# Weight sums in DRAM for fourteen pairs of the first MLP, and a later time for those of the second

## The chip, the cores and the metric

The kernel runs on one core of a Trainium2 chip. The metric is the device time of one execution in microseconds (us); the verdicts compare medians of runs. A core has a matrix engine (TensorE, PE in the profile), three engines for elementwise work (VectorE or DVE, ScalarE or ACT, GpSimd or POOL), a queue engine that issues transfers (SyncE or SP), and sixteen DMA engines that all queues share. Engines run their instructions in program order and wait for each other by semaphores.

## The reference, cut to what matters

Two decoder layers over 512 tokens of width 1024. Layer 0 mixes by a gated convolution beside differential attention, layer 1 by stick-breaking attention. Both then attend into 256 memory tokens and go through a gated MLP of inner width 2816 with a causal convolution of three taps.

```python
for l in range(DEPTH):                       # DEPTH = 2
    h = rmsnorm(x, norm_mix[l])
    x = x + (even_mixer(h, ...) if l % 2 == 0 else odd_mixer(h, ...))
    x = x + mem_attention(rmsnorm(x, norm_xattn[l]), rmsnorm(mem, norm_mem[l]), ...)
    x = x + conv_ffn(rmsnorm(x, norm_ffn[l]), ffn_w_up[l], ffn_conv[l], ffn_w_down[l])

def conv_ffn(h, w_up, w_conv, w_down):
    u = causal_dwconv(h @ w_up, w_conv)      # 1024 -> 2 * 2816
    gate, val = jnp.split(u, 2, axis=-1)
    return (jax.nn.silu(gate) * val) @ w_down
```

All of it is float32.

## The kernel before

**Products.** Activations lie transposed in SBUF, eight chunks of 128 features by 512 tokens. A float32 product is made of three products of a rounded part (`hi`) and its rest (`lo`): hi x hi, hi x lo, lo x hi, each a matmul of 128 x 128 weights with 512 columns. Weights come from DRAM in slots of 128 x 1024 (512 KB). ACT casts a slot into `hi`, DVE subtracts to get `lo`; three raw slots (`raw`) and five of each part (`hi`, `lo`) can be held.

**Pairs in the MLP.** The up-projection goes in 22 pairs, U0 to U21: column block j of the gate and block 22 + j of the value, 8 chunks deep. As whole matmuls a pair takes 2 x 8 x 3 = 48 of 512 columns. For the pairs in `SEVEN` the pair is cut into 2 x 2 blocks (two column blocks by odd and even chunks, and the tokens in two halves) and made of seven products instead of eight (`lin_halved`), each of 12 matmuls with 256 columns: 84. The sums of the token halves are made once per MLP (`fold`). The sums of the weight blocks are made in one of two ways:

- on DVE (`prep_halved`, last part): two slots are loaded, `a` and `r`; four additions of 128 x 512 in the raw slots (L454) give the sums, and the seven left operands are split from there.
- in DRAM, for the pairs in `SUMMED` (`sums_in_dram`): SP's queue copies the pair's four blocks from `wts` to a buffer `dr` in DRAM (1 MB); then three accumulating DMAs on POOL's queue (L508), each waiting for the one before, add blocks onto it. The pair is later loaded in four pieces (`halved_loads`): `a` (512 KB) and `d` (256 KB) from `wts`, `b` and `c` (512 KB each) from `dr`.

`SUMMED[l][j]` names a group of products: the sums of pair j of layer l may begin when the first column block of that group has been planned. In the kernel before, the second MLP has fourteen such pairs, with their sums between U8 of the first MLP and U1 of the second; the first MLP has none, and twelve pairs with DVE's sums. Pairs 12 and 14 of the first MLP are whole.

**Order of the work.** The program is written by a planner (`Issue`). Each piece of work is a generator with a priority; the planner keeps an estimated time for each engine and appends the operation that can start first. An engine's order is thus fixed at build time. Loads have priority 3.0 and the sums 6.0 (`SUMS`), the last. A transfer on SP costs the planner 0.5 us of SP, then 1.7 us, its bytes at 358 GB/s behind the transfers planned before, and 1.0 us. An accumulating DMA costs 1.0 us of POOL and lands 10 us later (`land`). It does not count as load on the DMA engines.

**POOL** also makes the inverse square roots (`rpow`, an operation with `mhalf`): of the norms, of the attention's heads and of the query norms. It clears small tiles in the stick-breaking attention.

**Order of groups**: V, QK0, A0, QK1, A1, A2 (input projection of layer 0 with its attention between), EO0, EO1 (its output projection), KV0 to KV3 (keys and values of the memory), Q0, Q1, XO0, XO1 (cross-attention), the MLP (`FFN_ORDER`: U0 to U21 with D00 to D21 of the down-projection between), then layer 1: SQK0, SV0, SQK1, SQK2, SV1, SQK3, SO0, the KV groups, SO1, Q0, Q1, XO0, XO1, MLP.

The lines of the profile: L492 is every matmul, L496 every transposition on PE, L439 ACT's copies and casts, L442 ACT's other operations, L454 two-input operations on DVE (and the root on POOL), L462 and L472 DVE's operations with scalars, L482 reductions, L501 every DMA on SP's queue, L508 the accumulating DMAs, L514 and L519 POOL's fills.

Of the kernel before, what the change touches and what calls it, by code (L numbers as in the profile page):

```python
# [36 lines left out]

UP_SCALED = 6
FFN_ORDER = [('u', 0), ('u', 1), ('u', 2), ('u', 3), ('u', 4), ('u', 5), ('u', 6), ('u', 7), ('d', 0, 0), ('u', 8), ('d', 0, 1), ('u', 9), ('u', 10), ('d', 0, 2), ('u', 11), ('u', 12), ('d', 0, 3), ('u', 13), ('u', 14), ('u', 15), ('u', 16), ('d', 1, 0), ('u', 17), ('d', 1, 1), ('u', 18), ('d', 1, 2), ('u', 19), ('u', 20), ('d', 1, 3), ('u', 21), ('d', 2, 0), ('d', 2, 1)]
SEVEN = {0: (8, 9, 10, 11, 13, 15, 16, 17, 18, 19, 20, 21), 1: (8, 9, 10, 11, 12, 13, 14, 15, 16, 17, 18, 19, 20, 21)}  # L40

SUMMED = {0: {}, 1: {8: 'U8_0', 9: 'U10_0', 10: 'U12_0', 11: 'U14_0', 12: 'U16_0', 13: 'U18_0', 14: 'U20_0', 15: 'SQK0', 16: 'SQK1', 17: 'SQK2', 18: 'SQK3', 19: 'Q0_1', 20: 'XO0_1', 21: 'U1_1'}}


def weight_groups():
# [61 lines left out]
LOW7 = {GN[n] for n in ()}  # L107
ADDED = {GN[f"U{j}_{l}"]: GN[after] for l in SUMMED for j, after in SUMMED[l].items()}
HALVED = {GN[f"U{j}_{l}"] for l in SEVEN for j in SEVEN[l]}
NSLOT = [len(g[3]) * len(g[4]) * P // SLOT for g in GROUPS]  # L110
# [279 lines left out]
def trunk(ctx: ExitStack, tc: tile.TileContext, xT: bass.AP, memT: bass.AP, wts: bass.AP, par: bass.AP, outT: bass.AP):  # L390
# [1072 lines left out]
    def ffn(l, xin, xout, last):  # L1463
# [40 lines left out]
        def up_done(j):  # L1504
            def done(m, ps):
                gate = m % 2 == 0
                u = ps
                if j < UP_SCALED:
                    u = yield AL(pC)
                    yield Until(lambda: "rrow" in N)  # L1510
                    yield tt(u, ps, N["rrow"], ALU.mult)
                    free(ps)
                t = yield AL(pG)
                yield from conv3(u, f"ffn_conv{l}", j if gate else 22 + j, 44, t)
                free(u)
                if gate:
                    yield act(t, t, AF.Silu)
                    gate_t[j] = t
                    F["silu", l] = F.get(("silu", l), 0) + 1
                else:  # L1520
                    yield Until(lambda: j in gate_t)
                    yield tt(t, t, gate_t[j], ALU.mult)
                    free(gate_t[j])
                    if 4 <= j < 16 or j > 19:
                        q = pHS if j < 16 else pG
                        hi, lo = yield [AL(q, F32R), AL(q, F32R)]
                        o, w = (hi, lo), (hi, lo)
                    else:
                        y = yield AL(pH, F32R, (P, 2, S))
                        o, w = (y[:, 0, :], y[:, 1, :]), (y,)  # L1530
                    yield from split(o[0], o[1], t)
                    free(t)
                    own[j] = w
                    acts[j] = o
            return done

        def up(j):
            done = up_done(j)
            if j in SEVEN[l]:
                acc = yield AL(aACC)  # L1540
# [329 lines left out]
```

## Time and profile before

| | |
|---|---|
| median of 3 runs | 1476.64 us (1476.16 to 1477.26) |
| profiled execution, and its span | 1476.87 us, 1475.1 us |
| busy in the span: PE, DVE, ACT, POOL | 1467.7, 1145.3, 786.4, 103.0 us |
| DMA packets moved | 186.74 MB, mean 127 GB/s |
| of them by accumulating DMAs (queue q0) | 14.68 MB, 6.4% of the sixteen engines' time |
| first halved product to last down-projection, MLP 0 and MLP 1 | 219.0 and 217.4 us |

Busy times of engines overlap. A wait is put down to the semaphore that came last. Rows of the chain or of a timeline begin with the start and the duration in us; rows of groups end with the busy time, the mean of one in ns and the idle time of the engine before them. A `q` behind an engine's name is its sequencer. The granted clock was full (1.00) in the stretches that are used here.

### The profile page before, as it was taken

Reading aid. Unit: us, or ns where it says so; the run is one execution under the profiler, and the core shown is the slowest. Engines: PE = TensorE matmul, PEld = TensorE weight load, DVE = VectorE, ACT = ScalarE, POOL = GpSimd, SP = SyncE. Lnnn points to the kernel's source line nnn. Section 1 sums busy time; section 2 is a strip of 40 time slices with the busy share of each in tenths; the row PEclk is TensorE's granted clock in tenths of the full one; section 3 lists DMA queues with packets and bytes.
Section 4 is the critical chain, followed back from the end, with each engine's and each line's share of the span. In section 5 each row is a group of like instructions: output and inputs, shape, how many; then the busy total and the mean of one; then the engine's idle time right before and its main releaser. Section 6 shows DMA issues by size and latency. Waiting matters only on the chain.

```text
span 1475.1 us, 20895 instructions
## 1 busy us (share of the span) xinstructions
PE 1467.7 (100%) x7904; PEld 1267.0 (86%) x7904; DVE 1145.3 (78%) x1923; ACT 786.4 (53%) x1303; POOL 103.0 (7%) x181
## 2 busy tenths in 40 slices
PE   9999999999999999999999999999999999999998
PEld 7888888888888989999888888888888889999897
DVE  7689766665898887888778989967657996888683
ACT  6576446453554344444577877855535653545341
POOL 2210000000000010000011111001000000000000
PEclk9999999999999999999999999999999999999999
DMA  7122445311333565656334443353244433455351
GB/s 237 58 86 73 131 141 172 114 58 58 100 101 128 133 170 156 171 147 196 129 88 127 116 133 81 132 183 107 86 125 140 126 110 124 145 160 179 124 165 57
DMA packets 63492, 186.74 MB, mean 127 GB/s; under 512 B 6208, under 2 KB 6720, under 8 KB 63168
## 3 DMA queue, kind: packets, MB, share of 16 engines
q1 hardware_dynamic: 55552, 170.73, 35.1%
q0 software_dynamic: 7840, 14.68, 6.4%
q8 instruction: 62, 1.02, 0.3%
q14 instruction: 38, 0.31, 0.1%
HBM read 183.29 MB, written 31.46 MB: 146 GB/s over the span
## 4 chain that ended last, share of the span: by engine, by line
PE 93%; DVE 3%; ACT 2%; DMA 1%; issue 1%; SPq 0%; DVEq 0%; ACTq 0%
PE acc L492 69%; PE sc L492 11%; PE pv L492 5%; PE tr L492 5%; PE tr L496 3%; DMA raw<-wts 1%; DVE lo L454 1%; DMA x<-xT 0%; ACT h L439 0%; ACT g L442 0%; DVE h L454 0%; DVE c L454 0%; SPq L501 0%; DVE g L454 0%; DVE g L1619 0%
## 5 line engine op out<-in xcount | busy, mean ns | idle before, releaser
L492 PE MATMUL acc<-hs,hi 128*128 128x512 f32 x1568 | 494.5, 392 | 0.0
L439 ACT CAST hi<-raw 128x1024 fp32r<-128x1024 f32 (+1 forms) x290 | 299.3, 1039 | 209.8 <-PE acc L492 79.6
L454 DVE TENSOR_TENSOR lo<-raw,hi 128x1024 fp32r<-128x1024 f32 (+1 forms) x290 | 347.5, 1205 | 73.6 <-ACT hi L439 71.3
L492 PEld LDWEIGHTS acc<-hs,hi 128*128 128x128 f32 x1568 | 292.7, 188 | 57.7
L492 PE MATMUL acc<-hs,lo 128*128 128x512 f32 x784 | 307.3, 392 | 0.0
L492 PE MATMUL acc<-h,hi 128*128 128x512 f32 (+1 forms) x648 | 187.2, 372 | 0.0
L492 PE MATMUL acc<-hi,hs 128*128 128x512 f32 x544 | 175.1, 394 | 1.0 <-ACT hs L442 1.0
L492 PEld LDWEIGHTS acc<-hs,lo 128*128 128x128 f32 x784 | 147.3, 188 | 28.6
L492 PEld LDWEIGHTS acc<-h,hi 128*128 128x128 f32 x648 | 117.8, 188 | 21.0 <-DVE x L454 0.3
L454 DVE TENSOR_TENSOR x<-x,acc 128x512 f32<-128x512 f32 (+1 forms) x105 | 71.0, 679 | 73.8 <-PE acc L492 73.3
L492 PE MATMUL acc<-h,lo 128*128 128x512 f32 (+1 forms) x324 | 119.7, 372 | 0.0
L492 PEld LDWEIGHTS acc<-hi,hs 128*128 128x128 f32 x544 | 101.0, 188 | 20.9 <-ACT hs L442 1.2
L462 DVE SCALAR_TENSOR_TENSOR g<-c,pp,g 128x510 f32<-128x510 f32 (+1 forms) x152 | 106.4, 744 | 0.9 <-ACT g L442 0.9
L492 PE MATMUL acc<-lo,hs 128*128 128x512 f32 x272 | 106.9, 394 | 0.0
L492 PE MATMUL acc<-y,hi 128*128 128x512 f32 (+1 forms) x328 | 90.9, 357 | 0.0
L492 PEld LDWEIGHTS acc<-h,lo 128*128 128x128 f32 x324 | 61.0, 188 | 10.7
L442 ACT ACTIVATE g<-c,pp 128x512 f32<-128x512 f32 x76 | 52.5, 720 | 27.4 <-DVE c L454 27.2
L492 PEld LDWEIGHTS acc<-y,hi 128*128 128x128 f32 x328 | 59.1, 189 | 9.3
L454 DVE TENSOR_TENSOR g<-g,g 128x512 f32<-128x512 f32 (+2 forms) x112 | 62.9, 568 | 4.4 <-ACT g L442 1.7
L442 ACT ACTIVATE g<-sc,rq 128x128 f32<-128x128 f32 (+7 forms) x128 | 61.2, 537 | 5.8 <-PE sc L492 5.4
L492 PEld LDWEIGHTS acc<-lo,hs 128*128 128x128 f32 x272 | 51.1, 188 | 10.0
L439 ACT CAST pt<-tr 128x128 fp32r<-128x128 f32 (+2 forms) x96 | 42.7, 455 | 30.5 <-PE tr L496 29.8
(241 smaller groups left out, 2500.9 us busy)
## 6 DMA issues: line engine op xcount, KB each, us to landing
raw<-wts SPq DMA_DIRECT2D x242, 512.0 KB, 4.0
raw<-dr SPq DMA_DIRECT2D x28, 512.0 KB, 3.7
dr<-wts POOLq DMA_DIRECT2D x14, 512.0 KB, 5.2
dr<-dr POOLq DMA_DIRECT2D x28, 256.0 KB, 4.1
raw<-wts SPq DMA_DIRECT2D x22, 256.0 KB, 3.2
x<-xT SPq DMA_DIRECT2D x16, 256.0 KB, 4.6
raw<-memT SPq DMA_DIRECT2D x4, 512.0 KB, 4.0
outT<-x SPq DMA_DIRECT2D x7, 256.0 KB, 2.0
```

The lines of the kernel that those rows point to most:

```text
L439: return nc.scalar.copy(out=out.ap, in_=in_.ap)
L442: return nc.scalar.activation(out=out.ap, in_=in_.ap, func=func, scale=_raw(scale), **kw)
L454: lambda: _ve(eng).tensor_tensor(out=out.ap, in0=in0.ap, in1=in1.ap, op=op))
L462: lambda: nc.vector.scalar_tensor_tensor(out=out.ap, in0=in0.ap, scalar=_raw(scalar), in1=in1.ap, op0=op0, op1=op1))
L492: lambda: nc.tensor.matmul(out.ap, lhsT.ap, rhs.ap, start=start, stop=stop))
L496: return Op("PE", 0.109, [in_, ident_v], [out], lambda: nc.tensor.transpose(out.ap, in_.ap, ident_v.ap))
```

## The change

Two tables change, and no function. `SEVEN[0]` gets pairs 12 and 14, so that fourteen pairs of the first MLP are made of seven products. `SUMMED[0]`, which was empty, names all fourteen: their sums are made in DRAM while the groups from A1 to XO1 of layer 0 run, and the pairs of the first MLP are loaded in four pieces like those of the second. `SUMMED[1]` gets other groups: the second MLP's sums begin at U17 of the first MLP instead of U8, and end at XO1 of layer 1. In several places two pairs name the same group, so two copies follow each other on SP's queue. The buffer `dr` grows from 14 to 28 places, since `pDR` has as many as there are pairs.

```diff
-SEVEN = {0: (8, 9, 10, 11, 13, 15, 16, 17, 18, 19, 20, 21), 1: (8, 9, 10, 11, 12, 13, 14, 15, 16, 17, 18, 19, 20, 21)}
-
-SUMMED = {0: {}, 1: {8: 'U8_0', 9: 'U10_0', 10: 'U12_0', 11: 'U14_0', 12: 'U16_0', 13: 'U18_0', 14: 'U20_0', 15: 'SQK0', 16: 'SQK1', 17: 'SQK2', 18: 'SQK3', 19: 'Q0_1', 20: 'XO0_1', 21: 'U1_1'}}
+SEVEN = {0: (8, 9, 10, 11, 12, 13, 14, 15, 16, 17, 18, 19, 20, 21), 1: (8, 9, 10, 11, 12, 13, 14, 15, 16, 17, 18, 19, 20, 21)}
+
+SUMMED = {0: {8: 'A1', 9: 'A2', 10: 'A2', 11: 'EO0', 12: 'EO0', 13: 'EO1', 14: 'KV1_0', 15: 'KV3_0', 16: 'Q0_0', 17: 'Q0_0', 18: 'Q1_0', 19: 'XO0_0', 20: 'XO0_0', 21: 'XO1_0'}, 1: {8: 'U17_0', 9: 'U19_0', 10: 'U21_0', 11: 'SQK0', 12: 'SQK0', 13: 'SV0', 14: 'SQK1', 15: 'SQK2', 16: 'SV1', 17: 'SQK3', 18: 'Q0_1', 19: 'Q1_1', 20: 'XO0_1', 21: 'XO1_1'}}
```

## The prediction

> **What bounds the kernel now.** I began with the page's busy times, then asked who TensorE (PE) waited for, then compared stages that the two layers have in common. The profiled execution took 1476.87 us with a span of 1475.1 us, so 1.77 us lie around the span; the median of the runs is 1476.64, 0.23 us below the profiled one. The sum below is made against 1476.87, and 0.23 is taken off at the end.
>
> ```profile
> span 1475.1 us, 20895 instructions
> PE 1467.7 (100%) x7904; PEld 1267.0 (86%) x7904; DVE 1145.3 (78%) x1923; ACT 786.4 (53%) x1303; POOL 103.0 (7%) x181
> ...
> PE pv L492 <- POOL pt L514: 1.1, 1, 1.1
> PE acc L492 <- ACT hs L442: 1.0, 1, 1.0
> PE sc L492 <- DVE s L1096: 0.5, 1, 0.5
> PE sc L492 <- ACT g L442: 0.3, 1, 0.3
> PE acc L492 <- ACT g L439: 0.3, 1, 0.3
> ```
>
> PE is idle for 1475.1 - 1467.7 = 7.4 us in all, and the list under it holds every wait of PE over the whole run: 3.2 us in five places. No other engine has work whose removal could be worth much: what is taken from DVE, ACT or the queues comes out of time in which PE runs anyway. The two MLPs, from the first product of a halved pair to the start of the last down-projection, and the two cross-attentions stand side by side in a table of stretches (PE, weight loads, DVE, ACT, POOL, granted clock, DMA share, GB/s):
>
> ```profile
> 473.20:692.20 219.00, 219.00 (x1441) 201.97 (x1440) 182.31 (x279) 96.98 (x128) 17.97 (x21) 1.00 0.59 166
> 1220.90:1438.30 217.40, 217.40 (x1513) 204.14 (x1512) 168.14 (x257) 101.89 (x135) 0.00 (x0) 1.00 0.49 152
> 259.30:374.20 114.90, 114.90 (x577) 97.44 (x576) 69.84 (x131) 50.83 (x94) 4.03 (x4) 1.00 0.22 73
> 1007.00:1121.90 114.90, 114.90 (x579) 97.34 (x578) 73.39 (x138) 52.05 (x96) 10.40 (x11) 1.00 0.38 110
> ```
>
> Rows 1 and 2: the first MLP is 219.00 us of 219.00 busy although DVE makes the sums in it (182.31 us of DVE work), and the second, whose sums come out of DRAM, is 217.40 of 217.40. So DVE's sums cost the first MLP nothing now. Row 2 is also what the first MLP becomes: same order of steps, fourteen halved pairs, all from DRAM.
>
> **The change, part by part.**
>
> *Two more pairs in seven products.* Pairs 12 and 14 of the first MLP go from 48 matmuls of 512 columns to 84 of 256 (seven products of twelve). From the chain in order of time (start, us, what):
>
> ```profile
> 661.32 1.44 PE acc L492 x12
> ...
> 1438.47 32.68 PE acc L492 x144
> ```
>
> A product is 1.44 us, so a halved pair is 7 x 1.44 = 10.08 us. 144 whole matmuls take 32.68 us, 0.2269 each, so a whole pair is 48 x 0.2269 = 10.89. Saved: 0.81 us a pair, **1.6 us** for two. The stretches say the same without any arithmetic on matmuls: 219.00 - 217.40 = 1.60. This is on the path and it is the only certain term.
>
> The Trainium skill (TensorE: Matmul & The Clock Gate, Back-to-back issue gap) gives N / 2.4 + 2.5 ns for an isolated warm matmul of N columns, 215.8 and 109.2 ns here; a pair would then save 48 x 0.2158 - 84 x 0.1092 = 1.2 us, two pairs 2.4, and the result would lie 0.8 us lower. The trace has 226.9 and 120.0 ns, a fixed part near 13 ns that the 84 short matmuls pay more often, so the trace's 1.6 is used.
>
> *DVE's sums go.* The four additions of each of the twelve pairs disappear:
>
> ```profile
> L454 DVE TENSOR_TENSOR raw<-raw,raw x36: 679/685/694, 461.7 to 681.2; 128x512 f32<-128x512 f32 x36
> L454 DVE TENSOR_TENSOR raw<-raw x12: 683/685/693, 462.4 to 679.3; 128x512 f32<-128x512 f32 x12
> DMA to landing us min/median/max: 2.5/3.8/7.4
> ```
>
> 48 x 0.685 = 32.9 us of DVE go; the splits and recombinations of the two new pairs come, and by rows 1 and 2 of the stretches some 182.31 - 168.14 = 14 us less remain in the whole. All of it lies under PE (row 1), so it is worth 0. The one place where it can come out is the joint behind the MLP, 700 to 725, where PE is short of the stretch by 0.30 us behind late weights:
>
> ```profile
> 686.46 7.37 DMA raw<-wts
> ...
> 682.46 0.84 POOL L508 DMA_DIRECT2D dr<-dr  x1 [4.71 <-DMA dr<-wts]
> 686.84 0.82 POOL L508 DMA_DIRECT2D dr<-dr  x1 [3.55 <-DMA dr<-dr]
> ...
> 700.00:725.00 25.00, 24.70 (x109) 19.81 (x108) 19.27 (x28) 15.46 (x23) 0.00 (x0) 1.00 0.26 85
> 825.00:850.00 25.00, 24.67 (x128) 20.12 (x128) 24.67 (x41) 21.72 (x43) 4.36 (x14) 1.00 0.49 127
> ```
>
> That 7.37 us landing, among the longest of the run (the 7.4 above), had the two last accumulations of a sum beside it. Bounds: 0 to -0.6 us (the idle time, and, as an estimate, as much again hidden inside pipelined matmuls); I take **-0.3**.
>
> *More loads in the first MLP.* Each pair is loaded in four pieces (1.75 MB) where two whole slots (1 MB) were. The second MLP does this at a DMA share of 0.49 with PE at 217.40 of 217.40: 0.
>
> *Fourteen more sums.* A sum is one copy of 1 MB from DRAM to DRAM on SP's queue and three accumulating DMAs on POOL's, each of which waits for the one before:
>
> ```profile
> dr<-wts POOLq DMA_DIRECT2D x14, 512.0 KB, 5.2
> dr<-dr POOLq DMA_DIRECT2D x28, 256.0 KB, 4.1
> dr<-wts SPq DMA_DIRECT2D x14, 6.1
> ...
> L508 POOL DMA_DIRECT2D dr<-dr x28: 805/822/884, 487.7 to 1152.5; - x28
> L508 POOL DMA_DIRECT2D dr<-wts x14: 878/888/1132, 481.9 to 1142.2; - x14
> ```
>
> Busy time of POOL: 14 x (0.89 + 2 x 0.82) = 35 us on an engine that is 7% busy. DMA time: rows 3 and 4 of the stretches hold the same cross-attention, the second with two whole sums in it: (0.38 - 0.22) x 114.9 / 2 = 9.2 us of all sixteen engines for one sum. PE's time there is 114.90 in both, so sums in a cross-attention cost **0**; six of the new ones go there (Q0, Q0, Q1, XO0, XO0, XO1) and four of the second MLP's.
>
> The other eight run where no sum has run yet, from A1 to the end of the cross-attention's keys and values:
>
> ```profile
> 110.00:150.00 40.00, 39.48 (x205) 33.08 (x204) 36.40 (x103) 24.98 (x59) 2.64 (x2) 1.00 0.21 69
> 150.00:213.00 63.00, 63.00 (x295) 52.40 (x294) 42.96 (x75) 30.19 (x49) 2.88 (x3) 1.00 0.39 127
> 213.00:259.00 46.00, 46.00 (x214) 38.04 (x213) 30.87 (x43) 26.62 (x44) 3.79 (x5) 1.00 0.55 183
> ```
>
> In 150 to 213 fall most of the sums behind A2 (two), EO0 (two) and EO1: about four, 37 us of DMA beside 0.39 x 63 = 25 us, which makes 62 of 63. The transfers there will queue, and one load has no cover (ACT's cast of the last weights of EO0, the PE group behind it):
>
> ```profile
> 169.32 0.33 SPq L501 DMA_DIRECT2D raw<-wts  x1
> ...
> 174.42 1.05 ACT L439 CAST hi<-raw 128x1024 fp32r<-128x1024 f32 x1 [2.08 <-DMA raw<-wts]
> ...
> 176.34 1.07 PE L492 MATMUL acc<-h,hi 128*128 128x512 f32 x4
> ```
>
> ACT idles 2.08 us for that load, casts until 175.47, and PE starts the products that need it 0.87 us later. A load beside sums took longer: the median was 4.5 us in the first MLP (sums beside it) and 3.9 in the second (none):
>
> ```profile
> raw<-wts SPq DMA_DIRECT2D x46, 512.0 KB, 4.5
> ...
> raw<-wts SPq DMA_DIRECT2D x33, 512.0 KB, 3.9
> ```
>
> So the stall at this place lies between 0 (0.6 us later, under 0.87) and 2.5 us (7.37 - 3.9 = 3.5 later, less 0.87 and rounded). The loads of EO1 right behind the two copies of EO0 stand alike, with some microseconds more cover. I take **+0.9** for the stretch, nearer the low end since the accumulating DMAs of a pair of sums come in three bursts and not at once; bounds 0 and 3.5.
>
> POOL is also the engine of the inverse roots, and a root behind a waiting accumulation waits with it; DVE, PE's transposes and the scores' scaling stand behind the root. The second cross-attention shows the two side by side:
>
> ```profile
> 1021.79 0.97 POOL L508 DMA_DIRECT2D dr<-wts  x1 [3.85 <-DMA dr<-wts]
> 1024.68 1.03 POOL L454 TENSOR_TENSOR k<-s,mhalf 128x4 f32<-128x4 f32 x1 [1.92 <-DVE s L472]
> 1027.37 0.88 POOL L508 DMA_DIRECT2D dr<-dr  x1 [1.66 <-DMA dr<-wts]
> ```
>
> The root at 1024.68 still waited for DVE, not for the accumulation: the planner puts 10 us between accumulations (`land`) where 4 to 5.5 pass, so roots fall in the gaps. 0, bounded above by one copy's lateness, 6.1 - 5.6 = 0.5 us at a place (5.6 is the planner's own 1.7 + 2.9 + 1.0).
>
> *The second MLP's sums are put later.* Three instead of seven run in the first MLP, seven instead of four in the stick-breaking attention. The only loss there that I can lay beside a sum is the 0.33 us of 825 to 850 (quoted above), inside which an accumulation was issued after a long wait:
>
> ```profile
> 830.18 0.88 POOL L508 DMA_DIRECT2D dr<-wts  x1 [5.09 <-DVE h L454]
> ```
>
> Three more sums at up to 0.66 (idle and as much hidden) give 0 to 2.0; I take **+0.2**.
>
> Sum: -1.6 - 0.3 + 0.9 + 0.2 = -0.8. 1476.87 - 0.8 - 0.23 = **1475.8 us**, -0.06%.
>
> **The rivals.**
>
> *Late weights decide (slower).* Place: EO0 and EO1, 169 to 200. If the copies and accumulations put the uncovered load 5 to 6 us back, PE stands 4 to 5 us there, and EO1's loads add 1 to 2. For it: 62 of 63 us of DMA; against it: the split tiles of five slots lie ready ahead of PE everywhere else, and no landing of the run passes 7.4 us. The result is above 1479.6 once the stalls pass 4.9 us (1.6 + 0.3 to eat up, 2.95 to lose); I put it at 1476.64 - 1.9 + 5.5 = 1480.2.
> The Trainium skill speaks for this rival (DMA: Bandwidth & Descriptors, Issuing engines are not separate DMA queues): transfers of SP and of POOL run on the same sixteen engines and interleave, so a sum on another queue is not out of the way. The 4.5 against 3.9 us agree.
>
> *DVE's relief counts (faster).* If the 33 us taken from DVE let the planner close the joints behind the first MLP and in the stick-breaking attention, at most the idle time found is to be had: 0.30 + 0.33, as much hidden, and 0.52 in 110 to 150, about 1.8 us: 1476.64 - 1.6 - 1.8 = 1473.2. Against it: 219.00 of 219.00.
>
> *A reordered stick-breaking attention.* DVE has 24.67 of 25 us there; a new order of POOL's work around seven sums costs 2 us more: 1477.3. Within 0.2%.
>
> *The two pairs gain nothing*, because their four loads come late and PE waits in the MLP: 1476.64. Against it: row 2.
>
> **How the numbers follow.** A measurement of this kernel can tell about 0.2% (2.95 us) from no change: below 1473.7 is faster, above 1479.6 slower. Forecast 0.54, reordered attention 0.14, no gain 0.05: all within, with a little of the relief rival, 0.74. Relief 0.10, nearly all of it faster: 0.09. Late weights 0.17: slower. The likeliest one's own range is 1474.4 (1476.64 - 1.6 - 0.6, no stall) to 1478.5 (1476.64 - 1.6 + 3.5). For 8 in 10 I go down to 1473.7 and up to 1479.4, which takes in 4.7 us of stalls beside the 1.9 saved.
>
> **What would show it.** Right: the stretch of the first MLP 1.6 us shorter with PE still full; DVE about 14 us less busy in it, to no effect; PE's list of waits unchanged but for short ones near EO0; landing times up in 150 to 213. Wrong: PE waits of several microseconds between 170 and 260 or around roots on POOL (late weights), or a shorter stretch anywhere but in the first MLP (relief).

## The result and the profile after

The changed kernel took 1483.86 us (median of four runs, 1478.99 to 1484.35) against 1476.45 us for the kernel before (1476.16 to 1477.26 on the same chip). The ratio is 1.0042, with a 95% interval of 1.003 to 1.0054: 0.42% slower. The prediction was 1475.8 us with a range that ended at 1479.4. The profiled execution is the fastest of the four, 2.1 us over the profiled execution of before; that the others are five microseconds slower still is part of what has to be explained.

The page of the changed kernel, busy times and the queue of the accumulating DMAs, and below it PE's longest wait, which the kernel before has too, with the waits that are new (engine and line, what it waited for: us in total, times, longest):

```profile
span 1477.2 us, 21209 instructions
PE 1467.9 (99%) x7976; PEld 1269.8 (86%) x7976; DVE 1125.6 (76%) x1893; ACT 787.0 (53%) x1309; POOL 139.4 (9%) x223
...
q0 software_dynamic: 15680, 29.37, 12.5%
```

```profile
PE pv L492 <- POOL pt L514: 1.1, 1, 1.1
PE tr L496 <- DVE pt L454: 0.9, 1, 0.9
PE tr L496 <- DVE nacc L454: 0.7, 1, 0.7
PE tr L496 <- DVE c L472: 0.6, 2, 0.4
PE acc L492 <- DVE c L454: 0.5, 2, 0.2
...
PE tr L496 <- DVE sq L454: 0.4, 1, 0.4
```

DVE lost 19.7 us of work and POOL gained 36.4, near the 35 that were worked out. PE is idle for 9.3 us where it was 7.4, and five kinds of waits are new: four of transpositions (`tr`) that wait for DVE, and one of products that wait for DVE's first operation of the norm behind XO1. The one on `sq` lies at 25 us, ahead of the first sum, and has nothing to do with the change.

Three stretches of the changed kernel (PE, weight loads, DVE, ACT, POOL, granted clock, DMA share, GB/s), the last from the first halved product of the first MLP to its last down-projection:

```profile
150.00:213.00 63.00, 63.00 (x295) 52.40 (x294) 42.96 (x76) 30.21 (x49) 12.43 (x14) 1.00 0.90 242
...
259.30:374.20 114.90, 113.61 (x568) 95.70 (x567) 67.59 (x128) 48.56 (x90) 20.48 (x23) 1.00 0.72 188
...
475.88:693.48 217.60, 217.60 (x1513) 204.19 (x1512) 168.28 (x257) 101.58 (x135) 5.14 (x6) 1.00 0.57 176
```

The MLP shrank from 219.00 to 217.60 us, still full, and DVE's work in it from 182.31 to 168.28. The stretch from 150 to 213, where the prediction looked for late weights, is full as well, at a DMA share of 0.90. Of these three stretches the loss is in the cross-attention: 114.90 of 114.90 before, 113.61 now.

To see where time comes and goes, the start of one and the same matmul in PE's order was taken from each trace and that of the trace before subtracted. Columns are the place in the trace before (us); values are us, positive is later. The first column only shows how the first loads of an execution vary. The labels are those of the experiments below. Three rows are not typical of their kernels: `after` is the fastest of four executions, `scratch` the fastest of eleven (1475.45 us, 1.6 under their median), `late` the slowest of nine (1485.21, 5.4 over it).

```
                 100    161    301    397    472    700    703    790   1145    end
after          +0.16  +0.17  +2.17  +2.69  +2.69  +1.27  +0.70  +1.65  +2.17  +2.17
again          -0.28  +1.14  +4.36  +4.88  +4.88  +3.26  +2.70  +4.10  +5.03  +5.03
unpaired       -0.13  -0.13  -0.13  +0.38  +0.38  -1.23  -1.80  -1.07  -0.32  -0.33
scratch        -0.74  -0.74  -0.29  +0.23  +0.23  -1.38  -1.95  -1.83  -1.35  -1.35
layer1_only    +0.05  +0.06  +0.06  +0.06  +0.06  +0.06  -0.51  -0.54   0.00   0.00
q0_split       -0.24  +0.87  +1.33  +1.86  +1.86  +0.24  -0.33  +0.86  +1.57  +1.57
late           +0.04  +0.06  +0.06  +0.12  +7.03  +8.73  +8.16  +7.95  +8.44  +8.44
seven_only     -0.53  -0.52  -0.52  -0.52  -0.52 +10.57 +10.89 +10.92 +10.92 +10.92
pairs_mlp      -0.02  -0.01  -0.01  -0.01  -0.01  +1.06  +0.67  +0.68  +0.67  +0.67
best           -0.23  -0.20  -0.21  -0.21  +0.43  +0.93  +0.36  +0.15  +0.12  +0.12
q0_pair        -0.29  -0.28  +2.94  +2.95  +3.77  +6.00  +5.43  +5.22  +5.22  +5.22
trim           -0.22  -0.22  -0.03  -0.02  -0.02  +1.37  +0.80  +0.59  +0.58  +0.58
apart          -0.42  -0.40  -0.40  -0.40  -0.40  -2.01  -2.58  -2.79  -2.77  -2.31
```

In the row of the changed kernel: +2.0 around the root of the first cross-attention (161 to 301), +0.5 at XO1 (397), -1.4 in the MLP, -0.6 in the joint behind it, +1.0 in the stick-breaking attention (703 to 790), +0.5 at XO1 of the second layer. The chain of waits of the changed kernel says what the first of these is (start, us, what; `issue` is time in which the engine waited for nothing that the profile shows):

```profile
264.63 9.01 DMA dr<-wts
273.64 5.42 issue
279.06 0.04 POOL dr L508
279.10 0.54 issue
279.64 1.40 POOL k L454
281.04 0.02 issue
281.06 0.17 DVE k L454
```

Q0 is named twice in `SUMMED[0]`. The copy of the second sum landed at 273.64. Its first accumulation is the next instruction on POOL and needs nothing else, yet it was issued 5.42 us later, at 279.06. Behind it on POOL stands the root (`k`, L454) that DVE, ACT's scaling and PE's transpositions wait for. In the kernel before the same root ran as soon as DVE had its input (POOL and DVE, timeline):

```profile
276.77 1.01 POOL L454 TENSOR_TENSOR k<-s,mhalf 128x4 f32<-128x4 f32 x1 [37.79 <-DVE s L472]
...
277.81 0.16 DVE L454 TENSOR_TENSOR k<-k,k 128x4 f32<-128x4 f32 x1 [1.12 <-POOL k L454]
```

So DVE's step is at 281.06 instead of 277.81. What POOL waited for in those 5.42 us shows when issue and landing of the accumulating DMAs are laid side by side (512 KB each, from the traces):

```
                 first issued   landed    second issued   after the landing
after               148.28      153.61       153.93            +0.32
again               148.79      156.29       156.61            +0.32
after               271.98      278.72       279.06            +0.34
again               274.17      280.93       281.26            +0.33
q0_pair             272.84      279.52       279.85            +0.33
scratch             147.62      155.70       149.89            -5.81
scratch             271.57      279.08       276.65            -2.43
```

A second accumulation of 512 KB is not issued until the first has landed, except in the kernel `scratch`, which gives POOL's DMA descriptors more room. In none of the twelve traces without that room are two of them under way at once. That is theory A of the experiments.

### The profile page after: what moved, and what is told of

The parts are those of the page before. It is cut to its first block, busy times and chain, and to the rows that moved or that the text cites. A ratio compares the mean times of both kernels' runs of the same rounds, so it can differ in the third digit from the quotient of the medians.

```text
span 1477.2 us, 21209 instructions
## 1 busy us (share of the span) xinstructions
PE 1467.9 (99%) x7976; PEld 1269.8 (86%) x7976; DVE 1125.6 (76%) x1893; ACT 787.0 (53%) x1309; POOL 139.4 (9%) x223
## 4 chain that ended last, share of the span: by engine, by line
PE 91%; DVE 3%; ACT 2%; DMA 2%; issue 1%; SPq 0%; POOL 0%; DVEq 0%; ACTq 0%
PE acc L492 65%; PE sc L492 12%; PE pv L492 6%; PE tr L492 5%; PE tr L496 3%; DVE lo L454 1%; DMA raw<-wts 1%; DMA dr<-wts 1%; ACT h L439 0%; ACT g L442 0%; ACT hi L439 0%; DMA x<-xT 0%; DVE h L454 0%; DVE c L454 0%; SPq L501 0%
## 5 line engine op out<-in xcount | busy, mean ns | idle before, releaser
L454 DVE TENSOR_TENSOR lo<-raw,hi 128x1024 fp32r<-128x1024 f32 (+1 forms) x292 | 350.7, 1205 | 87.1 <-ACT hi L439 85.5
L492 PE MATMUL acc<-h,hi 128*128 128x512 f32 (+1 forms) x624 | 179.1, 370 | 0.0
L454 DVE TENSOR_TENSOR x<-x,acc 128x512 f32<-128x512 f32 (+1 forms) x105 | 71.2, 680 | 79.7 <-PE acc L492 79.3
L492 PEld LDWEIGHTS acc<-h,hi 128*128 128x128 f32 x624 | 113.1, 189 | 19.4
L492 PE MATMUL acc<-h,lo 128*128 128x512 f32 (+1 forms) x312 | 114.6, 370 | 0.0
L462 DVE SCALAR_TENSOR_TENSOR g<-c,pp,g 128x511 f32<-128x511 f32 (+1 forms) x160 | 111.4, 744 | 0.0
L492 PE MATMUL acc<-y,hi 128*128 128x512 f32 (+1 forms) x304 | 82.6, 352 | 0.0
L508 POOL DMA_DIRECT2D dr<-wts x28 | 25.8, 921 | 445.0 <-DMA dr<-wts 409.3
L454 DVE TENSOR_TENSOR g<-g,g 128x512 f32<-128x512 f32 (+2 forms) x112 | 62.9, 568 | 4.6 <-ACT g L439 2.0
L492 PEld LDWEIGHTS acc<-y,hi 128*128 128x128 f32 x304 | 54.4, 189 | 8.1
```

Of the source, the lines that this page charges most:

```text
L454: lambda: _ve(eng).tensor_tensor(out=out.ap, in0=in0.ap, in1=in1.ap, op=op))
L462: lambda: nc.vector.scalar_tensor_tensor(out=out.ap, in0=in0.ap, scalar=_raw(scalar), in1=in1.ap, op0=op0, op1=op1))
L492: lambda: nc.tensor.matmul(out.ap, lhsT.ap, rhs.ap, start=start, stop=stop))
L508: lambda: nc.gpsimd.dma_start(out=out.ap, in_=i, accum_op=ALU.add, max_dma_last_dim=2048))
```

## The experiments

**The change again.** No edit; the question is how far the time spreads, and whether a slower execution shows longer landings in front of the same late roots.

> The changed kernel as it is, to see how far its time spreads. The profiled execution of it took 1478.99 us, three others 1483.39 to 1484.35. Theory A (pairs of sums): where a group is named twice, POOL stands at the second 512 KB accumulating transfer until the first has landed, and a root behind it is late; the stand is as long as the landing, 5.2 us at 148.28 us and 11.8 us at 186.19 us of the trace, so the time moves with the landings: 1478.5 to 1484.5 again, and an execution near 1484 shows longer landings ahead of the same late roots. Theory B (traffic): the copies and accumulations of 23 MB before the first MLP slow the weight loads, wherever the sums stand; the late ends are then at weight tiles, and more of them in an execution near 1484.

Measured: 1481.54 us (1480.64 to 1483.98), ratio 1.0031 (1.0021 to 1.0041). Its profiled execution is 2.9 us later at the end than the first one, and 1.0 us of it arises by 161 us. The 5.2 and 11.8 us in the expectation are the landings of the second accumulation of each pair; the first ones, for which POOL stands, took 5.3 and 7.5 us. Chain of waits of this execution, then POOL's timeline in the first execution of the same kernel at the same place:

```profile
148.79 0.89 POOL dr L508
149.68 6.91 issue
...
156.61 0.89 POOL dr L508
157.50 1.07 POOL s L454
...
158.60 0.17 DVE s L454
...
158.91 1.06 PE tr L496 x8
```

```profile
148.28 0.89 POOL L508 DMA_DIRECT2D dr<-wts  x1 [15.64 <-DMA dr<-wts]
153.93 0.90 POOL L508 DMA_DIRECT2D dr<-wts  x1 [4.77 <-issue]
155.17 1.03 POOL L454 TENSOR_TENSOR s<-s,mhalf 128x4 f32<-128x4 f32 x1 [0.35 <-DVE s L472]
```

The first accumulation of EO0's pair landed in 5.33 us there and in 7.50 here. In the one case POOL had been free for 0.35 us when the root began; in the other the input was ready at 154.6, the root began 2.6 us later, and PE stood for 1.2 us. So the loss here jumps with the landing time of one transfer, and the first profiled execution was no measure of the rest. At Q0 POOL stands equally long in both (5.4 us), but here the stand begins 1.2 us later relative to PE (2.2 us later in time, with PE 1.0 behind), and the stretch from 161 to 301 loses 3.2 us instead of 2.0.

**No group twice.**

```diff
-0: {8: 'A1', 9: 'A2', 10: 'A2', 11: 'EO0', 12: 'EO0', 13: 'EO1', 14: 'KV1_0', ..., 16: 'Q0_0', 17: 'Q0_0', ...}
+0: {8: 'A1', 9: 'A2', 10: 'EO0', 11: 'EO1', 12: 'KV1_0', 13: 'KV3_0', 14: 'Q0_0', 15: 'Q1_0', 16: 'XO0_0', 17: 'XO1_0', 18: 'U2_0', 19: 'U4_0', 20: 'U6_0', 21: 'U8_0'}
+1: {8: 'U17_0', 9: 'U19_0', 10: 'U21_0', 11: 'SQK0', 12: 'SV0', 13: 'SQK1', 14: 'SQK2', 15: 'SV1', 16: 'SQK3', 17: 'Q0_1', ..., 21: 'U1_1'}
```

> The same fourteen sums per MLP, but no group is named twice: the five doubled names of layer 0 and 1 are spread over neighbouring groups (A1, A2, EO0, EO1, KV1, KV3, Q0, Q1, XO0, XO1, U2, U4, U6, U8 of the first; U17, U19, U21 and the stick's and the second cross-attention's groups for the second). Theory A: no accumulation of 512 KB is issued while another is under way, the root of Q0_0 is not late, and the two pairs in seven products bring what they brought in the first MLP: 1475.0 to 1477.0 us. Theory B: about the same bytes ahead of the first MLP, ten sums in place of fourteen, so five sevenths of the loss stays: 1480 to 1483 us. Theory C (any sum in a cross-attention delays POOL's roots): Q0, Q1, XO0 and XO1 still have one each, so half or more of the loss stays: 1479 to 1482 us.

Measured: 1476.46 us, ratio 0.9993 (0.9984 to 1.0001). The loss is gone, and nothing moves between 100 and 301 us although ten sums still run ahead of the first MLP. Theories B and C fall. POOL around the root, with one sum in flight there:

```profile
273.12 0.88 POOL L508 DMA_DIRECT2D dr<-wts  x1 [4.80 <-DMA dr<-wts]
276.64 1.03 POOL L454 TENSOR_TENSOR k<-s,mhalf 128x4 f32<-128x4 f32 x1 [2.64 <-DVE s L472]
```

**More scratch for POOL's descriptors.** Pairs and all as in the change.

```diff
-    nc = bacc.Bacc("TRN2", ..., dynamic_dma_scratch_size=1024)
+    nc = bacc.Bacc("TRN2", ..., dynamic_dma_scratch_size=1216)
```

> The changed kernel with the scratch of POOL's own DMA descriptors at 1216 bytes in place of 1024, 19 more in the hundred, nothing else. Theory A, in the form that the second 512 KB accumulation finds no room for its descriptors: with enough room the second one of a pair is issued within 1 us of its copy and the time falls to 1475 to 1479 us; if 1216 bytes are still too little, the issue stays 0.3 us behind the landing of the first one and the time stays at 1478.5 to 1484.5. Theory B and C: no change, 1478.5 to 1484.5 us, also where the issue moves forward.

Measured: 1477.04 us, ratio 0.9999 (0.999 to 1.0008), on the same chip as the 1481.54 of the changed kernel. POOL at EO0 and, behind the dots, at Q0:

```profile
149.89 0.88 POOL L508 DMA_DIRECT2D dr<-wts  x1 [1.37 <-DMA dr<-wts]
...
271.57 0.90 POOL L508 DMA_DIRECT2D dr<-wts  x1 [4.20 <-DMA dr<-wts]
276.65 0.89 POOL L508 DMA_DIRECT2D dr<-wts  x1 [4.18 <-issue]
277.25 1.36 POOL L454 TENSOR_TENSOR k<-s,mhalf 128x4 f32<-128x4 f32 x1
```

With 192 bytes more, the second accumulation at EO0 waits for its copy alone. At Q0 it still stands, until 276.65; a third accumulation, issued at 266.56, landed at 276.34. The root is then at 277.25 instead of 279.64, though 0.9 us of that is the earlier start of this execution, and 0.45 us are lost between 161 and 301 instead of 2.0. So the limit is room in this scratch, and it is counted over everything in flight. The Trainium skill (DMA: Bandwidth & Descriptors, SWDGE vs HWDGE vs iDMA) says that GpSimd writes the descriptors of its DMAs into rings in a reserved part of SBUF, which the DMA engines drain, and that there is one such queue; this experiment agrees. How many descriptors a transfer takes there was not measured.

**Only the second MLP's sums moved** (`SEVEN` and `SUMMED[0]` as before, `SUMMED[1]` as changed).

> Only the second MLP's sums are moved to their later places (U17, U19, U21, the stick's, Q0, Q1, XO0 and XO1 of the second half); the first MLP has twelve pairs in seven products with the sums on DVE, as before. Theory A: the one doubled name left is SQK0; PE's wait of 1.1 us at 783.4 us of the trace stays: 1476.5 to 1478.5 us. Theory B: nothing is added before the first MLP, so 1476.0 to 1477.5 us. A third reading, that the loss comes from the sums moved into the stick attention and the second cross-attention, would give 1480 to 1484 us.

Measured: 1476.78 us, ratio 0.9997 (0.9989 to 1.0006). The loss does not come from there. The row of the table still shows two terms that go with these sums, -0.57 behind the first MLP and +0.53 at XO1. The expected wait of 1.1 us at 783 did not come; the part on the stick-breaking attention below has the load behind it.

**One name.** Pair 17's sum from Q0 to U2, all else as changed.

```diff
-16: 'Q0_0', 17: 'Q0_0',
+16: 'Q0_0', 17: 'U2_0',
```

> The changed kernel, with one name changed: pair 17's sum stands behind U2 and not behind Q0, so that the only pair that stood before the root of the first cross-attention is gone; the pairs at A2, EO0, XO0 and SQK0 stay. Theory A: the idle time of PE at 284 to 292 us of the changed kernel's trace (0.35, 0.59 and 0.83 us) and the late root at 279.64 us vanish: 1.5 to 3 us less, 1477.5 to 1480.5 us, what is left coming from the pair at EO0 when its landing is long. Theory B: one sum of fourteen less ahead of the first MLP, so 0 to 0.5 us less: 1480.5 to 1484 us.

Measured: 1478.62 us (1476.67 to 1479.01), ratio 1.0007 (0.9998 to 1.0016), as theory A had it: 2.9 us less than the 1481.54 of the changed kernel's longer series, for one sum of fourteen. (The two series come from two chips; the kernel before differs by 0.3 us between them.) Between 161 and 301 it loses 0.5, all of it at 244 us ahead of Q0, where the changed kernel lost 2.0 and 3.2. The pair at EO0 is still there, and costs 1.1 us at 161.

**Pairs where POOL has nothing to do.** The kernel before, with the first six sums of the second MLP named in pairs at U8, U12 and U16.

> The kernel before, with the first six sums of the second MLP named in pairs (U8, U12 and U16 of the first MLP twice each), where POOL has no root to form and the weights are loaded 10 us ahead. Theory A: POOL stands at the second accumulation here too, 5 to 8 us each, and it costs nothing, since nothing that PE waits for is behind it: within 0.5 us of the kernel before. Theory D (the two copies and accumulations at once are what costs, by late weight loads): 1478 to 1481 us, with PE idle at weight tiles near 540 to 650 us.

Measured: 1477.56 us, ratio 1.0008 (0.9999 to 1.0016). No root stands behind these, and no 3 us are lost. The median is 0.8 us over that of the kernel before, more than the 0.5 of theory A, but the interval takes in 1. PE's one new wait in the profiled execution, 0.8 us at 640 us, goes back over DVE to a weight that came late:

```profile
637.02 1.05 ACT L439 CAST hi<-raw 128x1024 fp32r<-128x1024 f32 x1 [3.04 <-DMA raw<-wts]
```

**Later, with nothing before XO0.**

```diff
+0: {8: 'XO0_0', 9: 'XO1_0', 10: 'U0_0', 11: 'U1_0', 12: 'U2_0', 13: 'U3_0', 14: 'U4_0', ..., 18: 'U8_0', 19: 'U10_0', 20: 'U12_0', 21: 'U14_0'}
+1: {8: 'U16_0', 9: 'U18_0', 10: 'U20_0', 11: 'SQK0', ..., 14: 'SQK3', 15: 'Q0_1', 16: 'Q1_1', 17: 'XO0_1', 18: 'XO1_1', 19: 'U1_1', 20: 'U3_1', 21: 'U5_1'}
```

> All fourteen sums of the first MLP stand behind XO0 and later (XO0, XO1, U0 to U8, U10, U12, U14), one each, and those of the second MLP one each from U16 of the first half on: nothing is added between A1 and Q1, where the unpaired kernel still has seven sums. Theory A (the loss was the pairs; single sums ahead of the first MLP cost nothing): the same as the unpaired kernel, 1475.5 to 1477 us. Theory B (the bytes added before the first MLP cost something too): below the unpaired kernel by more than 0.5 us, 1474 to 1476 us.

Measured: 1479.79 us (1477.28 to 1485.21), ratio 1.0024 (1.0013 to 1.0035). Both theories missed. No wait of PE in this execution has a root behind it. Instead the prediction's first rival, late weights, acts, and not at EO0 but in the first MLP. ACT, PE, and the stretch behind them, in the profiled execution:

```profile
471.41 1.04 ACT L439 CAST hi<-raw 128x1024 fp32r<-128x1024 f32 x1 [7.99 <-DMA raw<-dr]
...
473.03 0.80 PE L492 MATMUL acc<-hs,hi 128*128 128x512 f32 x1 [3.99 <-ACT hs L439]
...
473.00:478.00 5.00, 4.97 (x12) 3.92 (x13) 2.47 (x4) 1.04 (x1) 0.18 (x1) 0.50 0.97 184
```

The load that ACT waits for was issued at 461.42 and landed in 9.97 us; in the kernel with one sum a group, issued at 461.59, it took 3.62. Beside it ran the ends of two copies and three accumulations, and the sixteen engines were nearly full (0.83 of the time from 460 to 473, 0.97 in the row above, just behind it). PE pays 4.0 us for it, and then again: the granted clock is 0.50 for the next five microseconds. This is the slowest execution of the nine; the other eight had a granted clock of 0.999 or 1.000 over the whole span, so what the 3.0 us of the median are made of was not profiled.

**Only the two pairs.** `SEVEN[0]` with 12 and 14, sums on DVE and `SUMMED[1]` as before.

> Only the two more pairs in seven products (12 and 14 of the first MLP), their sums on DVE like the other twelve, and the second MLP's sums where they were. If the term of the prediction holds (1.6 us saved, less 1.4 us of idle time of PE at worst while DVE forms two more sums): 1475.2 to 1476.8 us. If the saving is lost again downstream, as the unpaired kernel's trace suggests (2.0 us ahead at the end of the first MLP, 0.3 us at the end): 1476.5 to 1477.5 us.

Measured: 1486.68 us, ratio 1.007 (1.0058 to 1.0082), ten microseconds slower than before; both expectations missed. PE's longest waits, the stretch from 560 to 605 us and two parts of it, and then the whole stretch in the kernel before (columns as above):

```profile
PE tr L492 <- DVE lo L454: 4.1, 3, 2.7
PE tr L492 <- ACT hi L439: 3.1, 1, 3.1
...
560.00:605.00 45.00, 37.85 (x275) 36.80 (x274) 39.78 (x66) 18.86 (x27) 3.37 (x4) 0.89 0.51 139
...
575.00:590.00 15.00, 11.36 (x75) 10.73 (x75) 14.86 (x24) 6.39 (x10) 1.71 (x2) 0.82 0.69 186
...
600.00:605.00 5.00, 3.33 (x16) 3.34 (x17) 5.00 (x7) 3.02 (x4) 0.00 (x0) 0.67 0.38 113
```

```profile
560.00:605.00 45.00, 45.00 (x308) 41.94 (x307) 39.48 (x64) 21.38 (x29) 3.43 (x4) 1.00 0.57 162
```

DVE had 39.5 of 45 us of work there already. With the sums of two more pairs it has no pause left where PE stands (14.86 of 15 us, 5.00 of 5) and becomes the engine that PE waits for. The waits come to 7.2 us; most of the rest goes with the lower clock behind the two longest (0.82 and 0.67 in the rows). So DVE's relief, worth 0 in the prediction, is a condition of the 1.6 us: without the sums in DRAM the two pairs cost ten.

**One sum a group, with the second MLP's early again.** Two of the smaller terms were to be taken out: the late weight at SV0, and the XO1 term. At XO1 the trace shows that the four transpositions of the norm's factor stand six matmuls later in PE's order, so DVE finds three accumulators waiting (x3) where it had found two, and PE waits for the last. DVE and PE in the changed kernel, then DVE in the kernel before:

```profile
393.40 1.89 DVE L454 TENSOR_TENSOR c<-acc,rrow 128x512 f32<-128x512 f32 x3 [3.32 <-ACT rrow L439]
...
394.15 0.73 PE L492 MATMUL acc<-hs,hi 128*128 128x512 f32 x2 [0.24 <-DVE c L454]
```

```profile
389.87 1.29 DVE L454 TENSOR_TENSOR c<-acc,rrow 128x512 f32<-128x512 f32 x2 [1.96 <-ACT rrow L439]
```

No sum stands at XO1, SV0 or SV1 in this kernel:

```diff
+0: {8: 'A1', 9: 'A2', 10: 'EO0', 11: 'EO1', 12: 'KV1_0', 13: 'KV3_0', 14: 'Q0_0', 15: 'Q1_0', 16: 'XO0_0', 17: 'U1_0', 18: 'U3_0', 19: 'U5_0', 20: 'U7_0', 21: 'U9_0'}
+1: {8: 'U10_0', 9: 'U12_0', ..., 13: 'U20_0', 14: 'SQK0', ..., 17: 'SQK3', 18: 'Q0_1', 19: 'XO0_1', 20: 'U1_1', 21: 'U3_1'}
```

> Sums for all fourteen pairs of the first MLP, one to a group: A1, A2, EO0, EO1, KV1, KV3, Q0, Q1, XO0, U1, U3, U5, U7, U9; those of the second MLP on U10 to U20 of the first, SQK0 to SQK3, Q0, XO0, U1 and U3 of the second half. No pair, none at XO1 (where the transposes of the norm's factor stood ten matmul groups later in PE's order and PE was 0.5 us later from then on), none at SV0. Theory A with its two smaller terms: 1.6 and 0.6 us saved in the first MLP as in the unpaired kernel's trace, and the 0.4 to 0.5 us at 392 and 1139 us and the 0.9 us at 781 us gone: 2.0 to 2.4 us under the kernel before, 1474.0 to 1475.5 us. If sums at the first MLP's own groups make weights late, as the sums at XO0 to U14 did (4.0 us of waiting at 473 us): 1477 to 1480 us.

Measured: 1476.91 us (1475.22 to 1478.5), ratio 1.0001 (0.9992 to 1.0009). That lies between the two ranges expected. The table shows the two terms gone (no step at 397 and 1145, no loss between 703 and 790), but +1.1 from 397 to 700 instead of -1.6. ACT's timeline:

```profile
590.22 1.05 ACT L439 CAST hi<-raw 128x1024 fp32r<-128x1024 f32 x1 [3.05 <-DMA raw<-wts]
```

Late weights again, at 589 and 597 us, with six sums of the second MLP running between U10 and U20. The kernel before had sums in the same places without a wait, but its pairs were loaded as two slots and not in four pieces; that this is the difference was not tested by itself.

**The pair at Q0 alone, added back** to the last kernel.

```diff
-14: 'Q0_0', 15: 'Q1_0',
+14: 'Q0_0', 15: 'Q0_0',
```

> The same with one name changed: the sum at Q1 stands at Q0, so that Q0 has two and no other group has. Theory A: POOL stands at the second accumulation until the first has landed, the root is 3 us later, PE is idle for 1.5 to 3 us at 284 to 292 us: that much over the kernel without the pair, 1476 to 1478 us. Any theory in which the count or the bytes of the sums matter: within 0.4 us of it.

Measured: 1482.40 us (1481.23 to 1484.62), ratio 1.0041 (1.0028 to 1.0054), a loss as large as that of the change, from one name. POOL:

```profile
272.84 0.88 POOL L508 DMA_DIRECT2D dr<-wts  x1 [4.71 <-DMA dr<-wts]
279.85 0.91 POOL L508 DMA_DIRECT2D dr<-wts  x1 [6.13 <-issue]
```

3.2 us arise between 161 and 301, as expected. The MLP loses 3.1 (397 to 700) where the kernel without the pair loses 1.1, with one wait more, 1.4 us at 542 us; why the MLP is worse for it was not found.

**Pairs with the larger scratch, without XO1 and SV0.** `SUMMED[0]` as changed save `21: 'U1_0'`, `SUMMED[1]` as in the kernel two experiments up, scratch 1216.

> The first MLP's sums as the change has them, pairs and all, save the last (U1 and not XO1), the second MLP's as in the kernel with one sum a group, and the scratch at 1216 bytes. Theory A: with room for the descriptors of two accumulations the pairs cost at most the 0.4 us seen at 289 us with 1216 bytes, and the two reorderings and the late weight are gone: 1474.0 to 1476.0 us. If more bytes early cost something by themselves: 1476 to 1478 us.

Measured: 1477.04 us, ratio 1.0000 (0.9991 to 1.0009). Expected 1474 to 1476; the pairs cost 0.2 us at 301, the reorderings are gone, and the MLP loses 1.4 instead of gaining 1.6, with the second MLP's sums at U10 to U20 as in the two kernels before this one. The time lies in the range expected if more bytes early cost something, but the loss is not early.

**The three lessons in one kernel.** One sum a group, none at XO1, SV0 and SV1, and only U17, U19 and U21 of the first MLP carry sums of the second.

```diff
+0: {8: 'A1', 9: 'A2', 10: 'EO0', 11: 'EO1', 12: 'KV1_0', 13: 'KV3_0', 14: 'Q0_0', 15: 'Q1_0', 16: 'XO0_0', 17: 'U0_0', 18: 'U2_0', 19: 'U4_0', 20: 'U6_0', 21: 'U8_0'}
+1: {8: 'U17_0', 9: 'U19_0', 10: 'U21_0', 11: 'SQK0', ..., 14: 'SQK3', 15: 'Q0_1', 16: 'Q1_1', 17: 'XO0_1', 18: 'U1_1', 19: 'U3_1', 20: 'U5_1', 21: 'U7_1'}
```

> One sum to a group, none at XO1, none at SV0 or SV1, and few of the second MLP's among the first MLP's own groups: A1, A2, EO0, EO1, KV1, KV3, Q0, Q1, XO0, U0, U2, U4, U6, U8 of the first, then U17, U19, U21, SQK0 to SQK3, Q0, Q1, XO0, U1, U3, U5, U7 of the second. If the first MLP keeps the 1.6 and 0.6 us that it gained with the sums at U17, U19 and U21 (unpaired kernel), and the three small losses (0.5 at XO1 twice, 0.9 at SV0) are gone as in the last kernels: 2.0 to 2.4 us under the kernel before, 1474.0 to 1475.5 us. If a weight of the first MLP is late here as well (0.8 and 1.2 us near 590 and 597 us with sums at U10 to U20): 1476 to 1477.5 us.

Measured: 1474.52 us (1474.05 to 1475.42), ratio 0.9985 (0.9976 to 0.9994) to the kernel before, 2.6 us under it and below the changed kernel in every execution. PE's whole list of waits in it, with nothing new but 0.2 us among the first loads:

```profile
PE pv L492 <- POOL pt L514: 1.1, 1, 1.1
PE sc L492 <- DVE s L1096: 0.4, 1, 0.4
PE sc L492 <- ACT g L442: 0.3, 1, 0.3
PE tr L496 <- DVE sq L454: 0.2, 1, 0.2
```

It has the same pairs in seven products, the same 28 sums and the same bytes as the change.

## Why the prediction was wrong, step by step

**Two more pairs in seven products, -1.6: right.** 219.00 to 217.60 in the changed kernel, and -1.61 between 472 and 700 in the unpaired kernel, the one with more scratch and the last one. The estimate from the Trainium skill (TensorE: Matmul & The Clock Gate, Back-to-back issue gap), 2.4 us for the two, is not what was measured.

**The joint behind the first MLP, -0.3: right in place, mis-sized.** It measured -0.57 in nearly every kernel, at the lower bound of -0.6. It came with the second MLP's sums alone too (0.06 to -0.51 in that kernel), where DVE still makes its sums, so DVE's relief is not needed for it. The load that had taken 7.37 us beside an accumulation, issued at 686.46, took 5.33 there, issued at 686.60, with none beside it.

**DVE's sums go, 0: right here, and incomplete.** That DVE's sums cost the first MLP nothing is true for twelve pairs; fourteen on DVE cost ten microseconds. The 1.6 us and the sums in DRAM are one edit, not two.

**Late weights at EO0 and EO1, +0.9: wrong in place.** In no kernel did PE wait there. ACT's idle time in front of EO0's last cast was 2.5 us where it had been 2.1, within the 0.87 us of cover that the prediction found. The load on the DMA engines that it forecast came (62 of 63 us forecast, a share of 0.90 measured), and did no harm in this stretch. The mechanism does exist: it took 4.0 us in the MLP with sums at XO0 to U14.

**Roots behind an accumulation, 0, at most 0.5 a place: this is the step that failed.** It read "the planner puts 10 us between accumulations (`land`) where 4 to 5.5 pass, so roots fall in the gaps". That holds for the three accumulations of one sum. Two sums that share a group don't wait for each other: the second one's first accumulation follows the first one's on POOL, and a root can come behind it in the order. The bound considered only a late copy. What decided is that POOL stands at the second accumulation until the first has landed: 5.4 us at Q0, a root 2.9 us late (276.77 to 279.64), 2.0 us of PE in one execution of the changed kernel, 3.2 in the other and in the kernel with that pair alone; and 0 to 1.4 us at EO0, depending on whether the landing before it took 5.3 or 7.5 us. The row that the step leaned on, from the second cross-attention of the kernel before, had one sum in flight. The sign that the prediction named, waits around roots on POOL, came: not one of several microseconds, but three of 0.2 to 0.7 us between 284 and 291 us in one execution, and up to 1.4 us in the other. The kernel before has no group with two, so its trace could not show this; a pair of names in the table was the sign that its rows did not cover the change.

**Sums in a cross-attention, 0: right for bytes and for single sums, wrong for the order.** The unpaired kernel has no loss from 161 to 301. But at XO1 the planner's order of PE changes with a sum there, and +0.5 at 397 and again at 1145 come from the norm's transpositions standing later. It depends on the order: in the kernel with late sums, which has one at XO1 too, they stand four matmuls later in the first layer and cost 0.06. The rows with "PE 114.90 in both" come from a kernel without a sum at XO1.

**The stick-breaking attention, +0.2 with a bound of 2.0: right in sign, mis-sized.** +1.2 and +1.6 in the two executions of the changed kernel, from 770 on (the table's 703 to 790 holds 0.2 that most kernels gain ahead of it). It is one load of weights. ACT and PE after, then ACT before:

```profile
780.25 1.05 ACT L439 CAST hi<-raw 128x1024 fp32r<-128x1024 f32 x1 [2.97 <-DMA raw<-wts]
...
783.40 0.55 PE L496 MATMUL tr<-ident,g 128*128 128x128 f32 x3 [0.95 <-DVE pt L454]
```

```profile
777.09 1.05 ACT L439 CAST hi<-raw 128x1024 fp32r<-128x1024 f32 x1 [0.30 <-DMA raw<-wts]
```

The load took 6.5 us where it had taken 3.8, issued 0.97 us behind an accumulation of 512 KB. With 1.04 us between the two it took 6.3 (unpaired), with 0.59 us 5.7 (more scratch, no wait of PE), with 0.56 us 7.0 (the changed kernel again), with 0.41 us 3.6 (only the second MLP's sums). The time does not follow the distance, and what lets the load through stays open.

The sum for the first profiled execution, from the table: +0.2 at the start, +2.0 at Q0, +0.5 at XO1, -1.4 in the MLP, -0.6 in the joint, +1.0 from there to 790, +0.5 at XO1 of layer 1: +2.2 at the end, against +2.1 in the times. For the second one, which is near the median of its series: -0.3 at the start, +1.4 at EO0, +3.2 at Q0, +0.5 at XO1, -1.6 in the MLP, -0.6 in the joint, +1.4 to 790, +0.9 behind it, +5.0 in all. Of what the prediction lacked there, 4.6 us are roots behind an accumulation.

**The rivals.** The one on the slower side had the size (1480.2) but not the cause; with its own cause it came true only in kernels that the change was not. The relief of DVE never showed. A reordered stick-breaking attention was half right: the reordering that cost was of PE at XO1.

**Open.** No execution of the changed kernel near 1484 us was profiled. Those at 1484.33 and 1484.35 had a granted clock of 0.997 and 0.998 over the whole span, that at 1483.39 one of 1.000. Five microseconds at half the clock, as in the kernel with late sums, would be 0.998 and 2.5 us; the two slowest of the kernel with the pair at Q0 alone (1484.28 and 1484.62) had 0.997 and 0.998 as well. That a longer stand behind a root leads to such a stretch is likely, and not shown.

## What to carry to other kernels

An engine that issues DMAs and also computes is a queue in which the small operation waits for the transfer's room: ask of every issue what stands behind it on that engine, how many transfers are then in flight, and whether the trace at hand ever had as many. When work that was spread one by one is named in pairs, rows of the spread kernel price a single one and no more. And slack is spent once: the first MLP could bear seven sums for the second beside it, or weights in four pieces for itself. With both, its loads came late in the four kernels that have sums between U10 and U16, and in none of the others.

## What the runs showed of the hardware that was not expected

A second accumulating DMA of 512 KB on POOL's queue was issued 0.32 to 0.34 us after the landing of the first, in the five places shown, in three traces, with 1024 bytes of scratch for its descriptors, and no two were under way at once in any of the twelve traces with that scratch; with 1216 bytes the second was issued while the first was under way. POOL shows no busy time in between: the row says "issue", and the engine's next instruction waits too.

A wait of PE of 4.0 us was followed by five microseconds at a granted clock of 0.50 (473 to 478 us, matmuls of 512 columns 0.43 us apart instead of 0.227), worth about 2.9 us more (the table's 6.9 between 397 and 472, less the 4.0). After each of PE's two long waits in the kernel with DVE's sums, 3.1 and 2.7 us, matmuls of 256 columns stand 0.21 us apart instead of 0.12 (587 to 591 and 602 to 605 us; the rows have 0.82 and 0.67). The waits of up to 1.4 us in the changed kernel lie in stretches at 1.00. The Trainium skill (TensorE: Matmul & The Clock Gate, What's actually happening) has the array's clock at half after an idle window of about 3.4 us. The waits of 4.0 and of 1.4 us agree with it; those of 2.7 and 3.1 us show that a shorter one can be enough here. The wait of 4.0 us cost this kernel 1.7 times its own time.
